# Row sums of a mixture of experts tied behind the last gate product, and three Hyena filters traced ahead of the projections

## The chip, the core and the metric

The kernel runs on one core of a Trainium2 chip. Its metric is the device time of one execution in microseconds (us): the median over several runs, beside one profiled execution whose trace is read below. Engines go by their short names: PE (TensorE, the matrix engine), DVE (VectorE), ACT (ScalarE), POOL (GpSimd), SP (SyncE, which issues most transfers).

## What is computed

Two layers of a trunk over 256 latent tokens (x) and 256 context tokens (xc), both 1024 wide. The layer's weights are shared by x and xc, and the modulation (six vectors from the conditioning c, through `ada_w`) differs between them. Cut to the parts that matter here:

```python
def _layer(x, xc, c, c_ctx, last, ...):
    sh1, sc1, g1, sh2, sc2, g2 = split(silu(c) @ ada_w + ada_b, 6)
    h = _rms(x, norm_mix) * (1.0 + sc1) + sh1
    q, k, v, hy, gates = _project(h, w_in, q_norm, k_norm)
    attn = _neighbourhood_attention(...)
    hyena = _hyena(hy, short_w, short_b, _hyena_filter_fft(L, flt_w1, ..., flt_w3), hy_skip)
    x = x + g1 * _merge(attn, hyena, gates, w_br_a, w_br_b, w_out)
    h2 = _rms(x, norm_ffn) * (1.0 + sc2) + sh2
    x = x + g2 * _hier_moe(h2, ...)          # 4 groups of 8 experts, top 1 group, top 2 experts
    if last: return x, xc                    # layer 1 needs of xc only keys and values
    ...                                      # the same for xc, with its own modulation

def _hier_moe(h, ...):                       # for each expert e and token t that it has
    y += (silu(h @ w1[e]) * (h @ w3[e]) * cw[t, e]) @ w2[e]
```

The Hyena filter does not depend on the tokens: a small sine network of the position, times a decay, normed over the positions, then a Fourier transform. There is one for each layer and order, (0,0), (0,1), (1,0) and (1,1).

## The kernel before, in words

All work is written by hand for the engines, in one program text that a tile library turns into one instruction stream for each engine. The order on an engine follows the place in the text, with a scheduler that moves an instruction past others when it is ready sooner; buffers come from numbered slots (`self.S(k, ...)`), and a transfer into a slot waits until the work on its last content is done.

**Start.** `build` loads constants and runs the filters' sine network (L1011), then loads eight 1 MB pieces of modulation weights (`ada_step`, L305): two at once, six inside `layer` through a ring of slots (L414). PE multiplies each piece with the conditioning as it lands (L316). `filter_load` (L1019) fetches the filters' weights, decay and Fourier table. `layer` then makes the rows of h: `head` (L441) squares x on ACT for its norm (L450), scales it (xn, L457), has PE transpose it (L461), ACT apply the modulation (hf) and DVE split it into a high and a low part (hT). `mm3` (L239 to L241) multiplies in three passes, high by high, low by high, high by low.

**A filter** (`filter`, L1035) has for each half of the positions two matmuls with decay (L1049, DVE hx), sums and differences (sf, half of them on POOL), splits (sd), absolute values (ACT) and their sum (ab, POOL), a norm matmul (L1063); then small matmuls for a reciprocal (L1069) and 24 three-pass matmuls of the Fourier transform, whose result H is stored to memory. Filter (0,0) stands behind `head`, the other three behind the projections of c = 0, 1, 2 (L550).

**The MoE** (`first_round`, L1373). Experts are worked on in 16 pairs. For a pair, `w13` (L1411) multiplies the pair's tokens with w1 and w3; `hidden` (L1359) makes the SiLU on ACT (sl), the gate product hd on DVE (L1365), a transpose on PE (L1368) and a copy on ACT (hdT); `w2` (L1426) follows. Weights stream in through rings of slots (`fetch`, L1390). The results of pairs 0 to 11 go out to rows of a buffer in memory (ybuf), the last four pairs' are put together by matmuls with a choice matrix (L1456). `collect(i)` (L1295) asks on POOL's queue for the two result rows of token tile i (yr or yt), and the function that it returns, `add`, sums them, multiplies by the modulation g2 and adds them to x, all three on DVE. Behind the first round stands a loop `overflow` for experts with more tokens than places; layer 1's head follows it.

The order around the change is set by the text, in `first_round`: half of the tiles is collected behind w2 of pair 12, their additions are written ahead of the second `hidden` from the end, and the other half is collected there and added at the end:

```python
            hdT = self.hidden(w13(2 * q, z["xT"], fill), z["cw"][:, 0:1])
            if q == 7:
                for u in adds:
                    u()
                adds = [collect(i) for i in range(nt // 2, nt)]
            ...
            if q == 6:
                adds = [collect(i) for i in range(nt // 2)]
```

## Time and profile before

| | us |
|---|---|
| median of 3 runs | 1447.03 (1446.01 to 1447.13) |
| the profiled execution | 1441.07 |
| its span in the trace | 1439.3 |
| busy: PE, DVE, ACT, POOL | 1281.0, 660.3, 455.8, 211.0 |
| first projection matmul starts | 59.39 |
| layer 0's MoE, last gate product | 867.42 |
| layer 1's first projection matmul | 893.28 |
| layer 1's MoE, last w2 starts | 1423.50 |

Times in a trace count from the span's start. The span is what the instructions of the core cover, the execution's own time lies 1.8 us over it. A row of a timeline has the start, the time, the engine (PEld is PE's weight load), the line, the operation, output and inputs; the brackets behind it tell how long the engine stood idle before it and what ended that. Matmuls are pipelined, so a row's time is longer than the distance to the next. A table by stretches gives busy time by engine, PE's granted clock as a share of 2.4 GHz, and the transfers' share of the 16 DMA engines.

### The profile page before, as it was taken

Reading aid. Unit: us, or ns where it says so; the run is one execution under the profiler, and the core shown is the slowest. Engines: PE = TensorE matmul, PEld = TensorE weight load, DVE = VectorE, ACT = ScalarE, POOL = GpSimd, SP = SyncE. Lnnn points to the kernel's source line nnn. Section 1 sums busy time; section 2 is a strip of 40 time slices with the busy share of each in tenths; the row PEclk is TensorE's granted clock in tenths of the full one; section 3 lists DMA queues with packets and bytes.
Section 4 is the critical chain, followed back from the end, with each engine's and each line's share of the span. In section 5 each row is a group of like instructions: output and inputs, shape, how many; then the busy total and the mean of one; then the engine's idle time right before and its main releaser. Section 6 shows DMA issues by size and latency. Waiting matters only on the chain. (4 is left out here: it accounts for less than half of the span.)

```text
span 1439.3 us, 18183 instructions
## 1 busy us (share of the span) xinstructions
PE 1281.0 (89%) x7071; PEld 831.1 (58%) x7071; DVE 660.3 (46%) x1361; ACT 455.8 (32%) x884; POOL 211.0 (15%) x175
## 2 busy tenths in 40 slices
PE   5999999999999999599888397999899969998776
PEld 2555777886578887344333134899779943443222
DVE  4654366676677666601000137865774760100014
ACT  3433223337632133222211014533574522221101
POOL 2021033361000000211110000032500021110000
PEclk9999999999999999699999699999999979999989
DMA  9744625455177762799999963325326749999991
GB/s 377 282 166 185 230 90 190 159 219 215 59 262 274 288 241 98 278 408 420 419 420 422 403 274 137 129 106 211 136 94 219 259 161 380 418 419 420 422 407 69
DMA packets 65691, 373.04 MB, mean 259 GB/s; under 512 B 11994, under 2 KB 13338, under 8 KB 26048
## 3 DMA queue, kind: packets, MB, share of 16 engines
q1 hardware_dynamic: 54368, 347.67, 61.9%
q0 software_dynamic: 10368, 21.02, 4.1%
q10 hardware_dynamic: 864, 3.15, 0.5%
q8 instruction: 57, 0.93, 0.3%
q14 instruction: 34, 0.28, 0.1%
HBM read 362.06 MB, written 27.53 MB: 271 GB/s over the span
## 5 line engine op out<-in xcount | busy, mean ns | idle before, releaser
L1411 PE MATMUL pW<-we,xT 128*64 128x512 f32 x1024 | 263.0, 605 | 8.5 <-DMA we<-in_wexp_dram 8.4
L1411 PEld LDWEIGHTS pW<-we,xT 128*64 128x64 f32 x1024 | 82.3, 138 | 149.8 <-issue 131.7
L239 PE MATMUL pA<-hT,wsp 128*128 128x512 f32 (+1 forms) x448 | 156.3, 349 | 4.0 <-ACT hf L223 4.0
L1365 DVE SCALAR_TENSOR_TENSOR hd<-sl,cws,pW 128x256 f32<-128x256 f32 x32 | 15.3, 480 | 305.9 <-ACT sl L223 305.9
L241 PE MATMUL pA<-hT,wsp 128*128 128x512 f32 (+1 forms) x448 | 154.4, 345 | 1.1 <-DVE wsp L220 1.1
L240 PE MATMUL pA<-hT,wsp 128*128 128x512 f32 (+1 forms) x448 | 154.0, 344 | 0.0
L220 DVE TENSOR_TENSOR wsp<-win,wsp 128x1024 fp32r<-128x1024 f32 x80 | 102.1, 1281 | 105.8 <-ACT wsp L223 105.6
L1426 PE MATMUL pW<-we,hdT 128*64 128x512 f32 x512 | 142.0, 621 | 4.9 <-ACT hdT L223 4.7
L223 ACT ACTIVATE wsp<-win 128x1024 fp32r<-128x1024 f32 x80 | 84.1, 1057 | 141.9 <-PE pA L241 137.2
L240 PE MATMUL pA<-wsp,hT 128*128 128x256 f32 x352 | 99.9, 284 | 2.6 <-DVE wsp L220 2.6
L239 PE MATMUL pA<-wsp,hT 128*128 128x256 f32 x352 | 100.2, 285 | 0.7 <-ACT vv L223 0.7
L241 PE MATMUL pA<-wsp,hT 128*128 128x256 f32 x352 | 99.7, 283 | 0.0
L239 PEld LDWEIGHTS pA<-hT,wsp 128*128 128x128 f32 x448 | 86.2, 192 | 21.6 <-issue 8.0
L240 PEld LDWEIGHTS pA<-hT,wsp 128*128 128x128 f32 x448 | 86.1, 192 | 13.7 <-issue 6.1
L241 PEld LDWEIGHTS pA<-hT,wsp 128*128 128x128 f32 x448 | 85.9, 192 | 11.1 <-issue 1.8
L1426 PEld LDWEIGHTS pW<-we,hdT 128*64 128x64 f32 x512 | 48.6, 141 | 73.3 <-issue 59.2
L223 ACT ACTIVATE Y<-pW 128x512 f32<-128x512 f32 (+1 forms) x64 | 38.2, 597 | 137.0 <-PE pW L1426 134.7
L223 ACT ACTIVATE sl<-pW 128x256 f32<-128x256 f32 x32 | 12.3, 383 | 218.7 <-PE pW L1411 218.7
L248 POOL TENSOR_TENSOR rs<-rsq,mh 128x1 f32<-128x1 f32 x14 | 8.4, 601 | 424.9 <-DVE rsq L247 414.0
L239 PEld LDWEIGHTS pA<-wsp,hT 128*128 128x128 f32 x352 | 67.3, 191 | 5.3 <-issue 2.5
L240 PEld LDWEIGHTS pA<-wsp,hT 128*128 128x128 f32 x352 | 67.4, 191 | 3.4 <-DVE wsp L220 3.2
L241 PEld LDWEIGHTS pA<-wsp,hT 128*128 128x128 f32 x352 | 67.4, 191 | 0.2
(301 smaller groups left out, 2324.4 us busy)
## 6 DMA issues: line engine op xcount, KB each, us to landing
we<-in_wexp_dram SPq DMA_DIRECT2D x190, 1024.0 KB
win<-in_win_dram SPq DMA_DIRECT2D x40, 1024.0 KB
ada<-in_ada_dram SPq DMA_DIRECT2D x32, 1024.0 KB
ada<-in_adaj_dram SPq DMA_DIRECT2D x16, 1024.0 KB
wbr<-in_wbr_dram SPq DMA_DIRECT2D x8, 1024.0 KB
wout<-in_wout_dram SPq DMA_DIRECT2D x8, 1024.0 KB
ybuf<-zero SPq DMA_DIRECT2D x12, 512.0 KB
bc<-modd SPq DMA_DIRECT2D x12, 512.0 KB
```

The costliest lines, as they stand in the source:

```text
L220: (eng or self.nc.vector).tensor_tensor(out=out, in0=a, in1=b, op=op)
L223: self.nc.scalar.activation(out, in_, func, **kw)
L239: self.nc.tensor.matmul(out, lh, rh, start=start, stop=False)
L240: self.nc.tensor.matmul(out, lh, rl, start=False, stop=False)
L241: self.nc.tensor.matmul(out, ll, rh, start=False, stop=stop)
L248: nc.gpsimd.tensor_tensor(out=out, in0=t, in1=self.mh[:, : shape[1]], op=ALU.pow)
L1365: nc.vector.scalar_tensor_tensor(out=hd, in0=sl, scalar=cws, in1=pa[:, 256:512], op0=ALU.mult, op1=ALU.mult)
L1411: nc.tensor.matmul(pa[64 * e : 64 * e + 64, :], xT[:, kc, cs], wt[(2 * p + e, kc // 4)][:, kc % 4, :], start=kc == 0, stop=kc == KC - 1)
L1426: nc.tensor.matmul(py[64 * e : 64 * e + 64, :], hdT[:, fc, 64 * e : 64 * e + 64], wt[(2 * p + e, 2)][:, fc, hs], start=fc == 0, stop=fc == 1)
```

## The change

Five edits. (1) In `build`, the filters' loads come first, the eight modulation pieces get slots of their own, and filters (0,0) and (0,1) are traced ahead of `layer`; (1,0) follows layer 0's `head`, (1,1) the projections of c = 0. (2) The output of the squares, which nobody reads, goes into xn in place of a buffer `sqj`. (3) H is stored through POOL's queue. (4) In the MoE only tiles 0 and 1 are collected, behind w2 of pair 12 and at once; POOL makes their sum and the product with g2, and the addition to x on DVE is tied behind the last gate product (`issue_after(self.last_hd)`). (5) In layer 0, the rows of tiles 2 and 3 (context) are asked for behind the first round, and POOL sums and multiplies them behind layer 1's `head([0, 1])`; DVE adds them in `head([2, 3])`. Layer 1's weight ring is one slot shorter in its last pass, since yr now has slot 15.

```diff
@@ build
-        for s in (4, 5):
+        self.filter_load(14, 16, 15)
+        for s in (4, 5, 6):
             self.ada_step(s)
-        self.filter_load(14, 16, 15)
         self.xres = self.load_x(20, 21)
+        for s in (7, 8, 9, 0, 1):
+            self.ada_step(s)
+        self.filter(0, 0, (17, 19), 2, "A", "B", "C")
+        self.filter(0, 1, (12, 13), 3, "A", "B", "C")
@@ layer
-        aring, ai = [6, 7, 8, 9, 12, 4, 5], [0]
+        aring, ai = [7, 8, 9, 4, 5, 6], [0]
...
                 if not full and i > 1:
+                    self.tt(xs[1][:, i % 2, :], xs[1][:, i % 2, :], self.crows[i - 2][0], ALU.add)
...
-                    j = self.T4([P, D], name="sqj")
-                    self.act(j, x_, AF.Square, accum_out=ss[:, 0:1])
+                    self.act(xn[i // 2][:, i % 2, :], x_, AF.Square, accum_out=ss[:, 0:1])
...
             head([0, 1])
+            y0, y1, gc = self.crows[0]
+            first = nc.gpsimd.tensor_tensor(out=y0, in0=y0, in1=y1, op=ALU.add).ins
+            with self.tc.issue_after(first):
+                self.tt(y0, y0, gc, ALU.mult, nc.gpsimd)
+                y0, y1, gc = self.crows[1]
+                self.tt(y0, y0, y1, ALU.add, nc.gpsimd)
+                self.tt(y0, y0, gc, ALU.mult, nc.gpsimd)
         if full:
-            self.filter(0, 0, (17, 19), 12, "B", "B", "C")
+            self.filter(1, 0, (17, 19), 20, "B", "B", "C")
...
-        for o in range(1 if full else 2):
+        for o in range(2):
...
             if c < 3 and full:
-                self.filter(*((0, 1), (1, 0), (1, 1))[c], (17, 19), 20, "B", "B", "C")
                 if c == 0:
-                    self.skip_load(1)
-                    self.tt(sw[:, 8:12, :], ...)
-                if c == 2:
+                    self.filter(1, 1, (17, 19), 20, "B", "B", "C")
+                if c == 0:
                     aring[:] = [14, 16, 18, 17, 19, 20, 21]
@@ filter_load
         self.skip_load(0)
+        self.skip_load(1)
@@ filter
-        nc.sync.dma_start(self.Hd[l, o], H.rearrange("p x j c -> p (x j c)"))
+        nc.gpsimd.dma_start(self.Hd[l, o], H.rearrange("p x j c -> p (x j c)"))
@@ moe, collect
-            if full and i % 2 == 0:
-                yr = self.S(21, [P, 2, D], name="yr")
+                yr = self.S(21 if full else 15, [P, 2, D], name="yr")
...
+            self.tt(yt[0], yt[0], yt[1], ALU.add, nc.gpsimd)
+            self.tt(yt[0], yt[0], g2[:, 0, :], ALU.mult, nc.gpsimd)
             def add():
-                x_ = xm[i // 2][:, i % 2, :]
-                self.tt(yt[0], yt[0], yt[1], ALU.add)
-                self.tt(yt[0], yt[0], g2[:, i // 2, :], ALU.mult)
-                self.tt(x_, x_, yt[0], ALU.add)
+                x_ = xm[0][:, i, :]
+                with self.tc.issue_after(self.last_hd):
+                    self.tt(x_, x_, yt[0], ALU.add)
@@ moe, behind the overflow loop
+        if full:
+            gc = self.T4([P, D], name="gc")
+            nc.sync.dma_start(gc, self.modd[l, 3, 1:2, :].partition_broadcast(P)[:, 0, :])
+            self.crows = []
+            for i in (2, 3):
+                yr = self.S((17, 19)[i - 2], [P, 2, D], name="yc")
+                for k in range(2):
+                    nc.gpsimd.dma_start(yr[:, k, :], ybuf[(k * nt + i) * P : (k * nt + i) * P + P, :])
+                self.crows.append((yr[:, 0, :], yr[:, 1, :], gc))
@@ first_round
-            seq = [15, 18, 11, 13, 16, 21, 2, 3, 17, 19, 4, 5, 6, 7, 8, 9] * 6
+            seq = [15, 18, 11, 13, 16, 21, 2, 3, 17, 19, 4, 5, 6, 7, 8, 9] * 5
+            seq += seq[1:16] + [18]
...
-            if q == 7:
-                for u in adds:
-                    u()
-                adds = [collect(i) for i in range(nt // 2, nt)]
...
             if q == 6:
-                adds = [collect(i) for i in range(nt // 2)]
+                adds = [collect(i) for i in range(2)]
```

Lines of the changed kernel lie a few below those of before: L1049 is L1058, L1063 is L1072, L1365 is L1384, L535 and L537 are L546 and L548, L316 and L354 are L320 and L358, L461 is L465.

**DVE, layer 0's MoE, the last pairs.** Before, hd of pairs 11, 12 and 13 (yr and yt are collected rows, the Y between are pair 12's results):

```order
L1365 SCALAR_TENSOR_TENSOR hd_6036<-sl_6034,cws_5463,pW_5990 128x256
L220 TENSOR_TENSOR yr_6133<-yr_6133 128x1024
L220 TENSOR_TENSOR yt_6136<-yt_6136,yt_6137 128x1024
L1365 SCALAR_TENSOR_TENSOR hd_6122<-sl_6120,cws_5630,pW_6076 128x256
L220 TENSOR_TENSOR Y_6129<-pW_6143,Y_6129 128x512
L220 TENSOR_TENSOR Y_6129<-pW_6152,Y_6129 128x512
L1365 SCALAR_TENSOR_TENSOR hd_6185<-sl_6183,cws_5630,pW_6140 128x256
L220 TENSOR_TENSOR Y_6192<-pW_6229,Y_6192 128x512
```

and, up to the hd of pair 15 (x is the residual stream, bc the modulation g2):

```order
L220 TENSOR_TENSOR yr_6272<-yr_6272 128x1024
L220 TENSOR_TENSOR yr_6272<-yr_6272,bc_6130 128x1024
L220 TENSOR_TENSOR yt_6275<-yt_6275,yt_6276 128x1024
L220 TENSOR_TENSOR x_4407<-x_4407,yr_6272 128x1024
L220 TENSOR_TENSOR yt_6275<-yt_6275,bc_6130 128x1024
L220 TENSOR_TENSOR x_4407<-x_4407,yt_6275 128x1024
L1365 SCALAR_TENSOR_TENSOR hd_6333<-sl_6331,cws_5797,pW_6280 128x256
```

Now, hd of pairs 14 and 15 and what follows:

```order
L1384 SCALAR_TENSOR_TENSOR hd_6259<-sl_6257,cws_5793,pW_6226 128x256
L220 TENSOR_TENSOR Y_6266<-pW_6270,Y_6266 128x512
L220 TENSOR_TENSOR Y_6266<-pW_6279,Y_6266 128x512
L1384 SCALAR_TENSOR_TENSOR hd_6320<-sl_6318,cws_5793,pW_6267 128x256
L220 TENSOR_TENSOR x_4400<-x_4400,yr_6129 128x1024
L220 TENSOR_TENSOR x_4400<-x_4400,yt_6134 128x1024
L220 TENSOR_TENSOR Y_6329<-pW_6340,Y_6329 128x512
L220 TENSOR_TENSOR Y_6329<-pW_6347,Y_6329 128x512
```

Two row sums stood ahead of the hd of pair 12 and six row operations of tiles 2 and 3 ahead of that of pair 15; now no row sum is on DVE, and the two additions to x stand directly behind the hd of pair 15.

**PE, ahead of layer 0's first projection.** Before, the last rows ahead of it and its own first (xn is transposed, hT and wsp are the projection's operands):

```order
L316 MATMUL pD_513<-ada_511,cc 32x512 x3
L1049 MATMUL pB_533<-w_19_163,fl_72 128x512
L461 MATMUL pA_320<-cst,xn_230 128x128 x2
L461 MATMUL pA_320<-cst,xn_231 128x128 x2
L461 MATMUL pA_329<-cst,xn_230 128x128 x2
L461 MATMUL pA_329<-cst,xn_231 128x128 x2
L1049 MATMUL pB_551<-w_19_163,fl_72 128x512
L1049 MATMUL pB_555<-w_19_163,fl_72 128x512
L239 MATMUL pA_441<-hT_226,wsp_438 128x512
```

Now, the end of the modulation (ada is a piece of its weights, L358 transposes its result) and what follows it; the first projection stands twelve rows behind the last one shown, transposes, a norm matmul and four of the next modulation between:

```order
L1058 MATMUL pB_525<-w_15_148,fl_72 128x512
L1058 MATMUL pB_529<-w_15_148,fl_72 128x512
L320 MATMUL pD_161<-ada_210,cc 32x512 x4
L1058 MATMUL pB_547<-w_15_148,fl_72 128x512
L1058 MATMUL pB_551<-w_15_148,fl_72 128x512
L358 MATMUL pD_217<-cst,md_162 128x128 x4
L1072 MATMUL pC_524<-ab_541,cst 128x512
L239 MATMUL pB_582<-sd_523,ft_152 128x512
L240 MATMUL pB_582<-sd_523,ft_152 128x512
L241 MATMUL pB_582<-sd_523,ft_152 128x512
L239 MATMUL pB_590<-sd_523,ft_152 128x512
L240 MATMUL pB_590<-sd_523,ft_152 128x512
```

Before, filter (0,0) and the four L1049 of (0,1) stood ahead of the first projection. Now all of (0,0) and (0,1) does, and of (1,0) the four L1058, both L1072 and six three-pass matmuls.

**DVE and POOL, layer 1's head.** DVE around the halves of the first u, before and now (yc are rows of tiles 2 and 3):

```order
L220 TENSOR_TENSOR qraw_7190<-cst,prm_6640 128x128
L535 SCALAR_TENSOR_TENSOR u_6729<-pA_6704,prm_6640,u_6729 128x255
L247 TENSOR_SCALAR rsq_6930<-ss_5013 128x1
L220 TENSOR_TENSOR qraw_7190<-cst,prm_6640 128x2x16
L537 SCALAR_TENSOR_TENSOR u_6729<-pA_6704,prm_6640,u_6729 128x255
L220 TENSOR_TENSOR wsp_6804<-win_6349,wsp_6804 128x1024
```

```order
L220 TENSOR_TENSOR hT_6634<-hf_6669,hT_6633 128x256
L546 SCALAR_TENSOR_TENSOR u_6724<-pA_6699,prm_6631,u_6724 128x255
L220 TENSOR_TENSOR x_4403<-x_4403,yc_6625 128x1024
L548 SCALAR_TENSOR_TENSOR u_6724<-pA_6699,prm_6631,u_6724 128x255
L220 TENSOR_TENSOR wsp_6799<-win_6332,wsp_6799 128x1024
L220 TENSOR_TENSOR vS_6695<-pA_6753,vS_6695 128x2x128
L546 SCALAR_TENSOR_TENSOR u_6758<-pA_6728,prm_6631,u_6758 128x255
L220 TENSOR_TENSOR x_4403<-x_4403,rest_6403 128x512
```

POOL behind the overflow loop, now:

```order
L1375 DMA yc_6625<-ybuf_124 128x1024 x2
L988 DMA ft_7190<-in_fmain_dram 128x2048
L481 TENSOR_TENSOR yc_6625<-yc_6625 128x1024
L220 TENSOR_TENSOR yc_6628<-yc_6628 128x1024
L220 TENSOR_TENSOR yc_6625<-yc_6625,gc_6623 128x1024
L220 TENSOR_TENSOR yc_6628<-yc_6628,gc_6623 128x1024
```

The addition of tile 2's rows stands between the two halves of the first u, and waits there for POOL's third row operation; before, POOL had only loads there and no 128x1024 operation.

## Rows read from the trace of the kernel before

**Rows 1.** Stretches: us, busy PE, PEld, DVE, ACT, POOL; PEclk, DMA share, GB/s.

```profile
160.00:580.00 420.00, 412.33 (x2372) 318.78 (x2370) 275.80 (x524) 151.52 (x304) 68.69 (x46) 1.00 0.52 191
780.00:800.00 20.00, 10.14 (x41) 3.42 (x37) 0.00 (x0) 2.07 (x4) 3.18 (x5) 0.86 1.02 420
800.00:820.00 20.00, 6.55 (x19) 2.21 (x19) 3.19 (x4) 1.07 (x3) 0.54 (x1) 0.54 0.98 405
1360.00:1380.00 20.00, 6.19 (x20) 2.33 (x17) 1.62 (x2) 0.77 (x2) 1.70 (x3) 0.61 1.02 422
```

**Rows 2.** Timeline of layer 0's MoE, 790 to 813 (start, us, engine, line; idle before).

```profile
790.17 0.38 ACT L223 ACTIVATE sl<-pW 128x256 f32<-128x256 f32 x1 [6.55 <-PE pW L1411]
...
803.78 1.23 DVE L220 TENSOR_TENSOR yr<-yr 128x1024 f32<-128x1024 f32 x1 [28.20 <-DMA yr<-ybuf]
...
812.44 0.48 DVE L1365 SCALAR_TENSOR_TENSOR hd<-sl,cws,pW 128x256 f32<-128x256 f32 x1
...
812.97 0.69 PE L1368 MATMUL pX<-cst,hd 128*128 128x128 f32 x2 [22.84 <-DVE hd L1365]
```

**Rows 3.** Layer 0, pairs 12, 14 and 15: timeline of PE, then one stretch.

```profile
814.14 5.72 PE L1426 MATMUL pW<-we,hdT 128*64 128x512 f32 x16 [0.47 <-ACT hdT L223]
...
849.37 0.44 PE L1368 MATMUL pX<-cst,hd 128*128 128x128 f32 x2 [0.99 <-DVE hd L1365]
...
850.28 3.71 PE L1426 MATMUL pW<-we,hdT 128*64 128x512 f32 x16 [0.47 <-ACT hdT L223]
...
867.95 0.44 PE L1368 MATMUL pX<-cst,hd 128*128 128x128 f32 x2 [3.39 <-DVE hd L1365]
...
844.00:846.00 2.00, 2.00 (x12) 0.64 (x10) 0.00 (x0) 0.00 (x0) 0.00 (x0) 1.00 0.04 16
```

**Rows 4.** Layer 1, pairs 12 to 15: timeline of PE and its weight loads, one stretch.

```profile
1376.11 0.69 PE L1368 MATMUL pX<-cst,hd 128*128 128x128 f32 x2 [13.81 <-DVE hd L1365]
...
1378.18 5.40 PE L1426 MATMUL pW<-we,hdT 128*64 128x512 f32 x15
...
1385.47 0.20 PEld L1411 LDWEIGHTS pW<-we,xT 128*64 128x64 f32 x4 [0.25 <-DMA we<-in_wexp_dram]
...
1423.50 3.65 PE L1426 MATMUL pW<-we,hdT 128*64 128x512 f32 x16
...
1408.00:1410.00 2.00, 1.01 (x6) 0.34 (x6) 1.05 (x2) 0.42 (x2) 0.00 (x0) 1.00 0.24 92
```

**Rows 5.** Start: timeline of PE and DVE, one stretch, groups of PE from 60 to 160.

```profile
20.01 2.08 PE L1049 MATMUL pB<-w,fl 64*128 64x512 f32 x4
...
49.97 0.68 DVE L220 TENSOR_TENSOR H<-pB,skb 128x512 f32<-128x512 f32 x1
...
59.39 0.50 PE L239 MATMUL pA<-hT,wsp 128*128 128x512 f32 x1
...
10.00:59.30 49.30, 40.82 (x174) 18.28 (x172) 28.75 (x66) 18.56 (x36) 9.39 (x9) 0.97 0.88 353
...
112.08 0.39 PE L239 MATMUL pB<-sd,ft 128*128 128x512 f32 x1
...
113.22 0.39 PE L241 MATMUL pB<-sd,ft 128*128 128x512 f32 x1
...
L1063 PE MATMUL pC<-ab,cst 128*128 128x512 f32 x12 | 6.8, 645 | 4.9 <-POOL ab L220 4.9
```

**Rows 6.** Layer 1's head: POOL group, row loads, DVE's splits (min/median/max), timeline.

```profile
L220 POOL TENSOR_TENSOR c<-qraw 128x512 f32<-128x512 f32 x2 | 4.0, 2000 | 0.0
...
yt<-ybuf POOLq DMA_DIRECT2D x8, 512.0 KB, 11.4
...
L220 DVE TENSOR_TENSOR wsp<-win,wsp x20: 1211/1225/2322, 887.8 to 998.4; 128x1024 fp32r<-128x1024 f32 x20
...
886.45 1.42 DVE L457 TENSOR_SCALAR xn<-x,rs 128x1024 f32<-128x1024 f32 x2 [0.58 <-DVEq L1350]
...
898.55 0.48 DVE L535 SCALAR_TENSOR_TENSOR u<-pA,prm,u 128x255 f32<-128x255 f32 x1 [0.94 <-ACT u L223]
```

More of the change, by code (lines that the diff above doesn't have):

```diff
@@ L543, in layer @@
             if c < 3 and full:
-                self.filter(*((0, 1), (1, 0), (1, 1))[c], (17, 19), 20, "B", "B", "C")
                 if c == 0:
-                    self.skip_load(1)
-                    self.tt(sw[:, 8:12, :], sw[:, 8:12, :], self.rn[0][:, 1, :].unsqueeze(2).to_broadcast([P, 4, 4]), ALU.mult)
-                if c == 2:
+                    self.filter(1, 1, (17, 19), 20, "B", "B", "C")
+                if c == 0:
                     aring[:] = [14, 16, 18, 17, 19, 20, 21]
@@ L1364, in hidden @@
         hd = self.TH([P, 256], name="hd")
-        nc.vector.scalar_tensor_tensor(out=hd, in0=sl, scalar=cws, in1=pa[:, 256:512], op0=ALU.mult, op1=ALU.mult)
+        self.last_hd = nc.vector.scalar_tensor_tensor(out=hd, in0=sl, scalar=cws, in1=pa[:, 256:512],
+                                                      op0=ALU.mult, op1=ALU.mult).ins
         ptt = self.ps("X", [P, 2, P])
```

## Prediction

> **What bounds the kernel now.** I read the page first: PE is by far the busiest engine, so time can come only from PE's gaps. The table by stretches shows where these are: PE is at 412.3 of 420 us from 160 to 580, but has 10.1 of 20 us from 780 to 800, 6.6 of 20 from 800 to 820 and 6.2 of 20 from 1360 to 1380, with its granted clock at 0.54 and 0.61 of 2.4 GHz there, close to the 1.2 GHz level [rows 1]. Then I read what ended each gap. In layer 0's MoE, ScalarE had the SiLU of pair 12 at 790.55, but DVE's gate product hd came only at 812.44: two 128x1024 sums stand ahead of it in DVE's order, and waited for rows that GpSimd had asked for (28.20 us for the first). PE stood 22.84 us for that hd [rows 2]. Layer 1 repeats it up to 1376.11, where PE stood 13.81 us [rows 4]. Last comes what the transfers allow: they run at 1.02 of their share through both gaps [rows 1], so weights keep arriving while PE stands, and that limits how far PE can move up.
>
> **B, the tail of layer 0's MoE.** The change takes every sum and product of MoE rows off DVE's order ahead of hd: at pair 12 nothing is left in front, and the last pair's six operations (two tiles, three each) are no longer there either. Three savings:
> - the wait itself, 22.8 us [rows 2];
> - half clock after it: w2 of pair 12 took 5.72 us, that of pair 14 3.71 [rows 3], so 2.0;
> - PE's wait for the last hd was 3.39 us against 0.99 at pair 14 [rows 3], so 2.4.
>
> Together 27.2. But the last hd cannot come before its weights. The transfer share is down to 0.04 in 844 to 846 [rows 3], so the last weights land near 845. The transfers were not standing in the gap, so I leave that time where it is. The transpose of the last hd then moves from 867.95 [rows 3] to about 846: **-22**. What PE could gain beyond, 5 us, becomes waits for weights.
>
> What it costs: the context rows (tiles 2, 3) are now asked for behind the routed part, two tiles summed and multiplied by GpSimd when layer 1 begins, and added to x by DVE between the two halves of layer 1's first u. That wait is new. Behind it on DVE are u's second half, a weight split and vS; PE waits for u with the transposes of projection 0, all its later projections standing behind them. The later pair of loads starts at about the loop's end, where the first xn stands (886.45 before), and lands 8 to 11 us later (11.4 is the median of yt) [rows 6], near 896. GpSimd has no 128x1024 sum in this trace; the longest of its 128x512 kinds takes 2.00 us [rows 6], so 2.0 to 4.0 at twice the columns; I take 3. The first needed product is the third in GpSimd's order: 896 + 3 x 3 = 905. Before, the u it splits stood at 898.55 [rows 6]. So DVE waits some 6 us there, of which PE can cover about a half with the next projection; DVE has 2.4 us fewer sums. I take **+3**, from -1 (the sums finish while xn and hT are made) to +8 (all of the wait reaches PE). Together **-19**, from -14 to -23.
>
> **C, the tail of layer 1's MoE.** The same sums leave DVE ahead of hd of pair 12: 13.8 us of wait, and 15 of the w2 matmuls behind it took 5.40 at half clock against 3.65 us for 16 of the last pair [rows 4]: 1.8. Sum 15.6. Against it stand the weights: at 1385.47 PE's load for pair 13 waited for a weight even in the delayed order [rows 4], and the share reaches 0.24 only in 1408 to 1410 [rows 4]. The last w2 ran from 1423.50; with weights in at about 1411 it can move by 12.5 at most. One row transfer more is put ahead of them (four row loads now go out together, against two at pair 12 and one at pair 13): 0.5 MB, 1.25 us at the 420 GB/s of those rows [rows 1]. **-11**, from -5 (a pair held twice by weights) to -12.5.
>
> **A, the start.** Three filters of Hyena are put ahead of the projections in the trace. By the order, filter (0,1) stands wholly ahead of the first projection matmul, of (1,0) its four decay matmuls, two norms and six three-pass matmuls; before, (0,0) stood there and four matmuls of (0,1). PE's price for one filter: four of L1049 at 1.04 (two, in four records, took 2.08), 4.2; two of L1063 at 1.13 (6.8 us for six), 2.3; 24 three-pass ones 0.23 apart (six starts from 112.08 to 113.22), 5.5; eight small ones of L1069 at the same spacing, 1.8 [rows 5]. That is 13.8. So 9.6 of (0,1) and 4.2 + 2.3 + 1.4 of (1,0), 17.5 us, pass from behind the first projection to ahead of it. They cost nothing where they fill PE's idle time there: 49.3 - 40.8 = 8.5 us between 10 and 59.3 [rows 5]. So the first projection moves from 59.39 by at least 9.0 us. At most it moves by 17.5 and the waits of filters with little beside them, which I bound by 5: three times a filter's share of PE's waits for the norm's input in 60 to 160, 4.9 / 3 [rows 5]. Of those 4.9 us, six norms of three filters, four norms leave: 3.3. So the sum is 9.0 - 20.8 = -11.8 at best and 22.5 - 20.8 = +1.7 at worst. I take a shift of 14.8, a little under the middle because matmuls of the modulation stand between the filters': **-6**.
>
> **Priced at nothing.** The square's output that goes into xn: ScalarE, same size. H's stores on GpSimd's queue in place of SP's: four issues of 1 MB, SP freed for weights. Loads of the modulation weights into slots of their own: the transfers before the first projection are the same bytes but for 0.5 MB of skip weights.
>
> **Sum.** -6 - 19 - 11 = -36. The profiled execution took 1441.07, so 1405. That execution lies 6.0 under the median of the runs, 1447.03; on that scale the time is **1411**.
>
> **A rule weighed.** What the row shows: the weight splits on DVE in layer 1's head take 1.225 us, and the longest of 20 took 2.322 [rows 6]. The Trainium skill's "SBUF — State Buffer", section "SBUF: two separate sides", says that a DVE operation with two SBUF inputs and a GpSimd operation that reads SBUF share one port pair, as a lock held for the whole instruction. The single long row agrees with such a lock, though it does not prove it. The time by such blocking is rival 3.
>
> **Rivals.**
> 1. *Weights bind both tails.* For: the wait of pair 13's load on a weight, and transfers at their full share. Every pair would stand a little for its weights, at the lower clock. Then B gives -12 and C -6: 1447 - 6 - 12 - 6 = 1423. Against: in layer 0 the last weights are in some 20 us before the last hd [rows 3]. Chance 0.14.
> 2. *The start gives nothing.* A filter is a chain PE, DVE, GpSimd and ScalarE, PE, and two more of them have only modulation matmuls to hide behind. A at +2: 1447 + 2 - 30 = 1419. Chance 0.13.
> 3. *GpSimd's sums block DVE in layer 1's head.* Four of 3 us make 12 us in which DVE's own sums and splits would stand still; with the 3 already counted, 8 to 9 more: 1419. For: the 2.322 us row. Against: the median split is 1.225, though GpSimd worked less there. Chance 0.12.
> 4. *Slower.* At the start the filters run as serial chains, each as long as (0,0) did: from 20.01 to its last H at 49.97, 30 us [rows 5]. Two more in a row move the first projection by 60, less the 20.8 that leave later stages: +39, against -30 of the tails: 1456. It decides from a first projection later than 110 us. Against: PE was at work 40.8 of 49.3 us there, on the modulation too. Chance 0.03.
> 5. *The sums still stand in front,* because the tie holds only what it names. Then only A stays, 1441, or nothing if A gives nothing. Against: the order has both x additions right behind hd of pair 15 and no row sum on DVE ahead of it. Chance 0.02.
>
> **How the numbers follow.** My forecast has 0.56. The low end takes all three parts at their best, -11.8 - 23 - 12.5 = -47, so 1400, and 3 for the measurement: 1397. The high end takes rival 1's 1423 and 3 more for it with a poor start: 1426. What a measurement can tell from no change is about 0.2%, 2.9 us. Slower is rival 4, 0.03; for no change I put rival 5's 0.02, though A alone would be a little faster; the rest, 0.95, is faster.
>
> **What would show it.** Right: hd of pair 12 half a microsecond behind its SiLU in both layers; PE's longest wait for hd under 3 us; no stretch from 780 to 820 under 15 us of PE; the last hd of layer 0 some 28 us earlier with the start's part, and end-of-weights waits of PE in place of the wait for hd; DVE standing about 6 us for a GpSimd product in layer 1's head; the first projection near 74. Wrong: PE waiting over 10 us for weights in either tail, a first projection past 82, splits on DVE over 2 us beside GpSimd's sums, or layer 1's first transposes of u more than 10 us behind the first projection.

## The result and the profile after

The changed kernel took 1423.62 us (median of 4 runs, 1421.39 to 1430.05), the kernel before 1446.52 beside it: ratio 0.9853, 95% interval 0.9817 to 0.9889. So it is faster by 1.5%, within the range forecast, but 12.6 us above the 1411 forecast. The profiled execution took 1422.41 us, 18.7 under the profiled one of before; the forecast sum was 36.

The page of the changed kernel, busy time by engine (us, share of the span, instructions):

```profile
PE 1278.2 (90%) x7071; PEld 832.5 (59%) x7071; DVE 652.4 (46%) x1349; ACT 457.3 (32%) x884; POOL 245.0 (17%) x191
```

PE has as much to do as before (1281.0), so the whole gain is idle time that went. Where it went is read by comparing starts of the same instruction in the two traces, the **lead**. First the stretches of the changed kernel (columns as in [rows 1]); the first and last belong to the start and layer 1's head:

```profile
10.00:79.40 69.40, 56.76 (x234) 27.14 (x235) 45.47 (x85) 30.54 (x56) 23.51 (x18) 0.98 0.74 292
...
780.00:800.00 20.00, 18.46 (x73) 6.74 (x71) 1.86 (x3) 3.65 (x7) 3.17 (x5) 1.00 1.01 419
800.00:820.00 20.00, 15.94 (x58) 5.39 (x55) 1.87 (x3) 1.96 (x4) 4.68 (x2) 1.00 1.01 411
...
860.00:880.00 20.00, 9.98 (x65) 8.46 (x64) 9.27 (x27) 5.95 (x11) 9.58 (x8) 0.82 0.54 193
...
1360.00:1380.00 20.00, 15.10 (x55) 5.06 (x55) 1.41 (x3) 1.97 (x4) 4.67 (x2) 0.91 1.02 418
```

The two holes of before are closed: PE has 18.5 and 15.9 us in 780 to 820 (10.1 and 6.6 [rows 1]) at full clock. A new hole stands in 860 to 880.

Timeline, the start, layer 0's tail and layer 1's tail of the changed kernel:

```profile
16.01 2.07 PE L1058 MATMUL pB<-w,fl 64*128 64x512 f32 x2 [3.77 <-ACT fl L223]
...
79.40 0.80 PE L239 MATMUL pA<-hT,wsp 128*128 128x512 f32 x1
...
790.91 0.38 ACT L223 ACTIVATE sl<-pW 128x256 f32<-128x256 f32 x1 [6.54 <-PE pW L1432]
...
791.33 0.48 DVE L1384 SCALAR_TENSOR_TENSOR hd<-sl,cws,pW 128x256 f32<-128x256 f32 x1 [15.01 <-ACT sl L223]
...
805.79 3.65 PE L1432 MATMUL pW<-we,xT 128*64 128x512 f32 x14 [2.59 <-DMA we<-in_wexp_dram]
...
844.85 0.44 PE L1388 MATMUL pX<-cst,hd 128*128 128x128 f32 x2 [0.99 <-DVE hd L1384]
...
1001.31 0.38 PE L240 MATMUL pA<-wsp,hT 128*128 128x256 f32 x1 [1.19 <-DVE wsp L220]
...
1352.91 0.38 ACT L223 ACTIVATE sl<-pW 128x256 f32<-128x256 f32 x1 [8.14 <-PE pW L1432]
...
1353.33 0.48 DVE L1384 SCALAR_TENSOR_TENSOR hd<-sl,cws,pW 128x256 f32<-128x256 f32 x1 [15.22 <-ACT sl L223]
...
1364.13 8.77 PE L1432 MATMUL pW<-we,xT 128*64 128x512 f32 x30 [3.33 <-DMA we<-in_wexp_dram]
...
1404.59 3.65 PE L1447 MATMUL pW<-we,hdT 128*64 128x512 f32 x16
```

Seven starts give the ledger (a positive lead is time by which the changed kernel is ahead):

| place (before, after) | lead | step |
|---|---|---|
| first projection (59.39, 79.40) | -20.0 | |
| SiLU of pair 12, layer 0 (790.17, 790.91) | -0.7 | start: 0.7 lost |
| last hd transposed, layer 0 (867.95, 844.85) | 23.1 | layer 0's tail: 23.8 gained |
| layer 1's first projection (893.28, 867.65) | 25.6 | 2.5 gained |
| an L240 matmul of wsp by hT (1013.50, 1001.31) | 12.2 | layer 1's head: 13.4 lost |
| SiLU of pair 12, layer 1 (1362.33, 1352.91) | 9.4 | 2.8 lost |
| last w2 (1423.50, 1404.59) | 18.9 | layer 1's tail: 9.5 gained |

The tails did what was forecast, and the start gave nothing. The loss is in layer 1's head. Its timeline in the changed kernel:

```profile
867.65 0.39 PE L239 MATMUL pA<-hT,wsp 128*128 128x256 f32 x1 [1.40 <-ACT hf L223]
871.43 0.48 DVE L546 SCALAR_TENSOR_TENSOR u<-pA,prm,u 128x255 f32<-128x255 f32 x1 [1.26 <-ACT u L223]
872.61 2.36 POOL L481 TENSOR_TENSOR yc<-yc 128x1024 f32<-128x1024 f32 x1 [8.31 <-DMA yc<-ybuf]
874.94 2.33 POOL L220 TENSOR_TENSOR yc<-yc 128x1024 f32<-128x1024 f32 x1
877.24 4.63 POOL L220 TENSOR_TENSOR yc<-yc,gc 128x1024 f32<-128x1024 f32 x2
879.60 3.35 DVE L220 TENSOR_TENSOR x<-x,yc 128x1024 f32<-128x1024 f32 x1 [7.68 <-POOL yc L220]
883.49 0.68 PE L524 MATMUL pA<-cst,u 128*128 128x128 f32 x2 [9.82 <-DVE u L548]
...
892.94 1.22 DVE L220 TENSOR_TENSOR x<-x,yc 128x1024 f32<-128x1024 f32 x1
```

Read it downwards. GpSimd's three operations in front of DVE's addition (two sums and the first of the two products in the row at 877.24) end at about 879.6; DVE has stood 7.68 us for them between the halves of u. The addition then takes 3.35 us beside GpSimd's second product, while the second addition (892.94), with no GpSimd work beside it, takes 1.22. Only then comes u's second half, and PE stands 9.82 us for it.

### The profile page after: what moved, and what is told of

It reads as the page before. It is cut to its first block, busy times and chain, and to the rows that moved or that the text cites. A ratio compares the mean times of both kernels' runs of the same rounds, so it can differ in the third digit from the quotient of the medians.

```text
span 1420.6 us, 18183 instructions
## 1 busy us (share of the span) xinstructions
PE 1278.2 (90%) x7071; PEld 832.5 (59%) x7071; DVE 652.4 (46%) x1349; ACT 457.3 (32%) x884; POOL 245.0 (17%) x191
## 5 line engine op out<-in xcount | busy, mean ns | idle before, releaser
L1432 PE MATMUL pW<-we,xT 128*64 128x512 f32 x1024 | 263.1, 605 | 16.3 <-DMA we<-in_wexp_dram 15.6
L1384 DVE SCALAR_TENSOR_TENSOR hd<-sl,cws,pW 128x256 f32<-128x256 f32 x32 | 15.4, 481 | 354.1 <-ACT sl L223 354.1
L240 PE MATMUL pA<-hT,wsp 128*128 128x512 f32 (+1 forms) x448 | 154.2, 344 | 0.0
L1447 PE MATMUL pW<-we,hdT 128*64 128x512 f32 x512 | 137.2, 598 | 4.9 <-ACT hdT L223 4.7
L240 PE MATMUL pA<-wsp,hT 128*128 128x256 f32 x352 | 100.5, 286 | 2.5 <-DVE wsp L220 2.5
L240 PEld LDWEIGHTS pA<-hT,wsp 128*128 128x128 f32 x448 | 86.2, 192 | 13.2 <-issue 5.5
L241 PEld LDWEIGHTS pA<-hT,wsp 128*128 128x128 f32 x448 | 86.1, 192 | 10.7 <-issue 1.3
L240 PEld LDWEIGHTS pA<-wsp,hT 128*128 128x128 f32 x352 | 68.2, 194 | 3.3 <-DVE wsp L220 3.1
```

The source lines that it names most:

```text
L240: self.nc.tensor.matmul(out, lh, rl, start=False, stop=False)
L241: self.nc.tensor.matmul(out, ll, rh, start=False, stop=stop)
L1384: self.last_hd = nc.vector.scalar_tensor_tensor(out=hd, in0=sl, scalar=cws, in1=pa[:, 256:512], op0=ALU.mult, op1=ALU.mult).ins
L1432: nc.tensor.matmul(pa[64 * e : 64 * e + 64, :], xT[:, kc, cs], wt[(2 * p + e, kc // 4)][:, kc % 4, :], start=kc == 0, stop=kc == KC - 1)
L1447: nc.tensor.matmul(py[64 * e : 64 * e + 64, :], hdT[:, fc, 64 * e : 64 * e + 64], wt[(2 * p + e, 2)][:, fc, hs], start=fc == 0, stop=fc == 1)
```

## Experiments

All are edits of the changed kernel ("after" below, 1423.62). Three groups ran beside the kernel before, at 1444.27, 1444.55 and 1446.40 us; ratios are against it, so they compare across groups. Differences in us below are of medians. Taken from the ratios, experiment 4 lies 6.7 us under after (7.6 by the medians), and experiments 7 and 9 lie 4.0 and 4.5 over 4 (4.8 and 5.1). First each part alone.

**1. The start undone:** filters, modulation slots, the squares' output and H's stores as before; tails and layer 1's head as changed.

```diff
@@ build
-        self.filter_load(14, 16, 15)
-        for s in (4, 5, 6):
+        for s in (4, 5):
             self.ada_step(s)
+        self.filter_load(14, 16, 15)
         self.xres = self.load_x(20, 21)
-        for s in (7, 8, 9, 0, 1):
-            self.ada_step(s)
-        self.filter(0, 0, (17, 19), 2, "A", "B", "C")
-        self.filter(0, 1, (12, 13), 3, "A", "B", "C")
...
```

> The change without its start: filters, modulation slots, the squares' output and H's stores as before; the MoE parts stay. Theory (the 17.5 us of filter work came to stand ahead of the first projection, but filled none of PE's idle time there, so the start is worth 0 to 2 us): first projection near 59.4 in place of 79.4, the tails and layer 1's head as in the changed kernel, time 1421 to 1427, within 3 us of the changed kernel's 1423.6. Rival (the start is worth the 6 us of the prediction and something else in layer 0 took them back): 1429 to 1431.

Measured: 1423.69 us, ratio 0.9857 (0.9841 to 0.9874), as the whole change. The start is worth nothing; the 20 us by which the first projection is later come back behind it, and no more.

**2. Layer 1's tail undone:** sums, products and additions on DVE again, called ahead of the second-last hidden.

```diff
@@ moe, collect
-            self.tt(yt[0], yt[0], yt[1], ALU.add, nc.gpsimd)
-            self.tt(yt[0], yt[0], g2[:, 0, :], ALU.mult, nc.gpsimd)
+            if full:
+                self.tt(yt[0], yt[0], yt[1], ALU.add, nc.gpsimd)
+                self.tt(yt[0], yt[0], g2[:, 0, :], ALU.mult, nc.gpsimd)
             def add():
                 x_ = xm[0][:, i, :]
+                if not full:
+                    self.tt(yt[0], yt[0], yt[1], ALU.add)
+                    self.tt(yt[0], yt[0], g2[:, 0, :], ALU.mult)
+                    self.tt(x_, x_, yt[0], ALU.add)
+                    return
@@ first_round
             if q == 7:
+                if not full:
+                    for u in adds:
+                        u()
...
```

> The changed kernel with layer 1's row sums, products and additions on DVE again, ahead of the second last gate product in the text, so that both sums stand ahead of hd of pair 12; layer 0 stays as changed. Theory (layer 1's tail is worth 9 to 10 us, and comes from this order alone): DVE waits for the rows ahead of hd of pair 12, PE stands 12 to 18 us there, time 9 to 13 us over the changed kernel, 1432 to 1437. Rival (weights bound that tail, the lead of 19 us at its end was the lead at its start): under 3 us, 1421 to 1427.

Measured: 1441.54 us (8 runs), ratio 0.998 (0.9969 to 0.9991), 18 over after. Timeline of this kernel, DVE and PE:

```profile
1370.87 1.23 DVE L220 TENSOR_TENSOR yr<-yr 128x1024 f32<-128x1024 f32 x1 [27.51 <-DMA yr<-ybuf]
1378.52 1.23 DVE L220 TENSOR_TENSOR yt<-yt,yt 128x1024 f32<-128x1024 f32 x1 [6.42 <-DMA yt<-ybuf]
1379.66 0.48 DVE L1390 SCALAR_TENSOR_TENSOR hd<-sl,cws,pW 128x256 f32<-128x256 f32 x1
...
1380.19 0.69 PE L1394 MATMUL pX<-cst,hd 128*128 128x128 f32 x2 [22.12 <-DVE hd L1390]
```

The row sums ahead of hd cost what PE waits for them. It is more than expected because two tiles are now asked for at once, so two sums stand there: the second waits another 6.42 us for its rows. In the kernel before it was one:

```profile
1374.43 1.23 DVE L220 TENSOR_TENSOR yt<-yt,yt 128x1024 f32<-128x1024 f32 x1 [26.72 <-DMA yt<-ybuf]
```

The rival, that weights hold this tail anyway, falls.

**3. Rows asked for later:** the four row loads go out from ScalarE's queue behind the SiLU of pair 13; the load of g2 stays where it was.

```diff
@@ moe, collect
             for k in range(2):
-                nc.gpsimd.dma_start(yt[k], ybuf[(k * nt + i) * P : (k * nt + i) * P + P, :])
+                with self.tc.issue_after(self.sls[-2]):
+                    nc.scalar.dma_start(yt[k], ybuf[(k * nt + i) * P : (k * nt + i) * P + P, :])
...
```

> The changed kernel with the row loads of the two tiles issued from ScalarE's queue behind the SiLU of pair 13 in place of behind w2 of pair 12, in both layers. Theory (2 MB of rows go ahead of the weights of pair 13, 5 us at 420 GB/s, and make PE's 3.3 us wait for weights and its lower clock in layer 1, 2.6 us in layer 0): both waits go under 1 us, time 3 to 6 us lower, 1418 to 1421. Rival (the end of all weights bounds the tails, rows and weights together take the same time in either order): within 2 us, 1421 to 1426.

Measured: 1423.39 us, ratio 0.9847 (0.9827 to 0.9867), no change. Timeline of PE in this kernel, layer 1, pairs 13 and 15:

```profile
1365.46 7.08 PE L1436 MATMUL pW<-we,xT 128*64 128x512 f32 x30 [0.88 <-DMA we<-in_wexp_dram]
...
1395.17 5.40 PE L1436 MATMUL pW<-we,xT 128*64 128x512 f32 x16 [4.24 <-DMA we<-in_wexp_dram]
```

The wait for weights at pair 13 went from 3.33 to 0.88 us and came back as 4.24 at pair 15. With the sums out of the way, the tail ends with the last transfer, whichever goes first: the rival held.

Now layer 1's head.

**4. The additions later:** both context additions are tied behind the last half of u of projection 3.

```diff
@@ layer, head
-                    self.tt(xs[1][:, i % 2, :], xs[1][:, i % 2, :], self.crows[i - 2][0], ALU.add)
+                    with self.tc.issue_after(self.last_u):
+                        self.tt(xs[1][:, i % 2, :], xs[1][:, i % 2, :], self.crows[i - 2][0], ALU.add)
@@ layer, behind the second half of u
...
+                if m < 4:
+                    self.last_u = last
```

> The changed kernel with the two additions of the context rows in layer 1's head tied behind the last half of u of projection 3, nothing else moved by hand. Theory (DVE's wait of 7.7 us for GpSimd's products, the 3.35 us addition beside a GpSimd product, and PE's 9.8 us and lower clock behind them are the 15 us that layer 1's head lost): PE's wait ahead of the first transposes of u goes from 9.8 to under 1.5, 8 to 12 us come back, time 1411 to 1416. Rival (the head's time comes back as a wait for weights in layer 1's MoE, or DVE's later work only moves behind the projections): at most 3 us, 1420 to 1424.

Measured: 1416.01 us (1414.3 to 1416.69), ratio 0.9807 (0.979 to 0.9823): 7.6 under after, and 7.7 under experiment 1, which ran in the same group. That is a little under the theory's 8 to 12 us, and far from the rival's 3. Timeline of PE, DVE and POOL in this kernel:

```profile
866.09 0.58 PE L239 MATMUL pA<-hT,wsp 128*128 128x256 f32 x1 [1.15 <-ACT hf L223]
...
872.06 2.52 DVE L220 TENSOR_TENSOR wsp<-win,wsp 128x1024 fp32r<-128x1024 f32 x1
...
873.47 3.38 POOL L220 TENSOR_TENSOR yc<-yc 128x1024 f32<-128x1024 f32 x1
...
875.62 2.31 DVE L220 TENSOR_TENSOR wsp<-win,wsp 128x1024 fp32r<-128x1024 f32 x1
...
878.97 2.31 DVE L220 TENSOR_TENSOR wsp<-win,wsp 128x1024 fp32r<-128x1024 f32 x1
...
887.62 0.48 PE L525 MATMUL pA<-cst,u 128*128 128x128 f32 x2 [1.74 <-DVE u L549]
894.93 1.12 PE L466 MATMUL pA<-cst,xn 128*128 128x128 f32 x4 [4.07 <-DVE rsq L247]
...
993.49 0.39 PE L240 MATMUL pA<-wsp,hT 128*128 128x256 f32 x1 [1.20 <-DVE wsp L220]
```

PE's wait for u fell from 9.82 to 1.74 us, so the place of the additions was the largest part of the head's loss. But from the first projection to the row at 993.49 the lead still falls from 27.2 to 20.0, and the weight splits on DVE now take 2.3 to 2.5 us beside GpSimd's work. Two suspects are left: that blocking, and DVE's load.

**5. All context row work on DVE:** as 4, but sums and products are on DVE too, tied at the same place.

```diff
@@ layer, head
...
+                    y0, y1, gc = self.crows[i - 2]
                     with self.tc.issue_after(self.last_u):
+                        self.tt(y0, y0, y1, ALU.add)
+                        self.tt(y0, y0, gc, ALU.mult)
                         self.tt(xs[1][:, i % 2, :], xs[1][:, i % 2, :], y0, ALU.add)
@@ layer, behind head([0, 1])
-            first = nc.gpsimd.tensor_tensor(out=y0, in0=y0, in1=y1, op=ALU.add).ins
...
```

> As the experiment with the additions tied behind the projections' u (1416.0), but sums and products of the context rows on DVE too, all tied there; GpSimd does no row work in layer 1's head. DVE has 4 x 1.22 = 4.9 us more to do in front of the context's xn. Theory (what that version still loses in layer 1's head, about 8 us of lead against the ends of the two tails, is DVE's chain in front of the context's xn): PE's wait for that xn grows from 4.1 by 2 to 5 us, time 1418 to 1421. Rival (the loss there is GpSimd's blocking of DVE's splits): no weight split in the head over 1.5 us, the wait does not grow, time 1413 to 1416.

Measured: 1417.16 us (1415.8 to 1421.4), ratio 0.9811 (0.9795 to 0.9827), the same as 4. Timeline of DVE and PE in this kernel:

```profile
871.80 1.23 DVE L220 TENSOR_TENSOR wsp<-win,wsp 128x1024 fp32r<-128x1024 f32 x1
...
874.95 1.23 DVE L220 TENSOR_TENSOR wsp<-win,wsp 128x1024 fp32r<-128x1024 f32 x1
...
878.12 1.23 DVE L220 TENSOR_TENSOR wsp<-win,wsp 128x1024 fp32r<-128x1024 f32 x1
...
894.80 1.11 PE L469 MATMUL pA<-cst,xn 128*128 128x128 f32 x4 [6.25 <-DVE xn L465]
...
899.28 1.12 PE L469 MATMUL pA<-cst,xn 128*128 128x128 f32 x4 [3.37 <-DVE xn L465]
```

The same three splits take 1.23 us each: the blocking is gone, as the rival said, and with it PE's 1.74 us for u. But PE's wait for the context's xn grew from 4.07 to 9.62 us (two waits), as the theory said. The time lies between the two forecasts, at neither. Stretch 880 to 900 in experiment 4 (columns as in [rows 1]):

```profile
880.00:900.00 20.00, 13.81 (x82) 11.43 (x81) 19.48 (x34) 9.42 (x21) 7.43 (x6) 0.83 0.49 174
```

and in experiment 5:

```profile
880.00:900.00 20.00, 10.38 (x69) 9.15 (x68) 19.46 (x31) 7.77 (x17) 3.47 (x3) 0.82 0.24 79
```

DVE is at work 19.5 of 20 us in both. In the kernel before, without the context's row work, a stretch 7 to 27 us behind the first projection (here it is 14 to 34) had DVE at 17.3 and PE at 18.5:

```profile
900.00:920.00 20.00, 18.52 (x142) 16.85 (x140) 17.30 (x39) 11.49 (x21) 0.00 (x0) 1.00 0.45 159
```

So DVE was nearly full here already, and work that is moved here costs, on DVE directly or on GpSimd through DVE's longer operations. No run takes the row work out of this head again, so that DVE's load makes the rest of the loss is inferred, not shown.

**6. Products on DVE:** as after, with the addition where the change has it, but the product with g2 on DVE ahead of it.

```diff
@@ layer, head
+                    y0, y1, gc = self.crows[i - 2]
+                    self.tt(y0, y0, gc, ALU.mult)
                     self.tt(xs[1][:, i % 2, :], xs[1][:, i % 2, :], self.crows[i - 2][0], ALU.add)
@@ layer, behind head([0, 1])
-                self.tt(y0, y0, gc, ALU.mult, nc.gpsimd)
                 y0, y1, gc = self.crows[1]
                 self.tt(y0, y0, y1, ALU.add, nc.gpsimd)
-                self.tt(y0, y0, gc, ALU.mult, nc.gpsimd)
```

> The changed kernel, but the products of the context rows with g2 are made on DVE, directly ahead of their additions; GpSimd only sums. In the changed kernel the two sums ended at 877.24 (layer 1's head), two GpSimd products of 2.3 us followed (both in a row of 4.63), and DVE's first addition stood from 879.60 for 3.35 us, against 1.22 for the second, which had no GpSimd work beside it. Theory 1 (DVE stands still while GpSimd works on two operands in SBUF): DVE's product starts when the first sum is there but is not done before the second sum ends, about 877.3 + 1.2; the addition then takes 1.22 and ends near 879.7 instead of 882.95, so PE's wait for u falls from 9.8 to about 6.6 us and the time by 3: about 1420.5. Theory 2 (no blocking, the addition was long for another reason): product from 875.0 at 1.2 us, addition done at 877.4, PE's wait about 4.3, time about 1418. Rival (what PE gains there it loses again waiting for the xn of the context tiles): time 1422 to 1424 with the shorter wait.

Measured: 1419.88 us (1417.36 to 1422.68), ratio 0.9824 (0.9808 to 0.984), as theory 1 forecast. Timeline of this kernel:

```profile
877.65 2.33 POOL L220 TENSOR_TENSOR yc<-yc 128x1024 f32<-128x1024 f32 x1
...
877.72 3.35 DVE L220 TENSOR_TENSOR yc<-yc,gc 128x1024 f32<-128x1024 f32 x1 [5.47 <-POOL yc L483]
...
881.33 1.21 DVE L220 TENSOR_TENSOR x<-x,yc 128x1024 f32<-128x1024 f32 x1
881.46 0.58 PE L240 MATMUL pA<-hT,wsp 128*128 128x256 f32 x1 [5.63 <-DVE hT L220]
```

The blocking moves with GpSimd: DVE's product, started 0.07 us behind GpSimd's second sum, takes 3.35 us, and the addition, now without GpSimd beside it, 1.21. Against the forecast, PE now stands for hT (5.63 us), which is queued behind the product, and not for u.

**7. Rows in another slot:** as 4, but tile 2's rows go into slot 12, so that they are loaded and summed ahead of the overflow loop, and the tie is one projection earlier.

```diff
-            first = nc.gpsimd.tensor_tensor(out=y0, in0=y0, in1=y1, op=ALU.add).ins
...
+            with self.tc.issue_after(self.last_row):
+                first = nc.gpsimd.tensor_tensor(out=y0, in0=y0, in1=y1, op=ALU.add).ins
...
-                if m < 4:
+                if m < 3:
...
-                yr = self.S((17, 19)[i - 2], [P, 2, D], name="yc")
+                yr = self.S((12, 19)[i - 2], [P, 2, D], name="yc")
...
```

> The kernel e3 with tile 2's rows in slot 12 in place of 17, which the overflow loop uses, so that they are asked for before the loop; both row sums on GpSimd are queued behind the row loads, ahead of the loop; the additions are tied behind u of projection 2. Theory (what is left of the head's loss is the chain from the context rows over the additions, the norm and xn to PE, where PE stood 4.1 us in e3): that wait falls under 1.5 us, time 1411 to 1414. Rival (the additions beside GpSimd's products take 2 to 3 us each by the lock, and give it back): within 1.5 us of e3, 1414.5 to 1417.5.

Measured: 1420.84 us, ratio 0.9835 (0.9815 to 0.9855), 4.8 slower than 4; both expectations fail. Timeline of this kernel:

```profile
852.81 2.40 POOL L483 TENSOR_TENSOR yc<-yc 128x1024 f32<-128x1024 f32 x1 [7.19 <-DMA yc<-ybuf]
853.05 4.38 DVE L220 TENSOR_TENSOR wsp<-win,wsp 128x1024 fp32r<-128x1024 f32 x2
...
865.10 1.42 DVE L462 TENSOR_SCALAR xn<-x,rs 128x1024 f32<-128x1024 f32 x2 [0.25 <-DVEq L1363]
...
870.97 4.86 POOL L220 TENSOR_TENSOR yc<-yc,gc 128x1024 f32<-128x1024 f32 x2 [3.15 <-DMA gc<-modd]
871.07 2.55 DVE L220 TENSOR_TENSOR hT<-hf,hT 128x256 fp32r<-128x256 f32 x1
873.54 2.64 DVE L230 CAST hT<-hf 128x256 fp32r<-128x256 f32 x2
```

The early sum sits beside two splits (4.38 us for both), and xn starts at 865.10 against 860.43 in 4. Of that, 2.3 us stood already at the SiLU of pair 12 in layer 0 (791.92 against 789.62), ahead of all that this edit moves, so some 2.4 us belong to it. The products sit beside the hT that PE needs at once, where the last addition of hT takes 2.55 us (0.42 elsewhere). Earlier rows gain nothing when GpSimd's work then lies beside DVE's critical one.

Last, three versions of the start, all with the additions later as in 4.

**8. The start undone** (edits of 1 and 4 together).

> The kernel e3 (additions of the context rows tied behind u of projection 3) with the start as before, too. Theory (the start is worth nothing by itself, also where layer 1's head no longer stands): within 3 us of e3's 1416.0, 1413 to 1419. Rival (the start is worth 6 us that layer 1's head had taken back): 1421 to 1423.

Measured: 1416.91 us, ratio 0.9807 (0.9782 to 0.9832), equal to 4. Again the start is worth nothing.

**9. Two modulation pieces ahead of the filters' loads.**

```diff
-        self.filter_load(14, 16, 15)
-        for s in (4, 5, 6):
+        for s in (4, 5):
             self.ada_step(s)
+        self.filter_load(14, 16, 15)
         self.xres = self.load_x(20, 21)
-        for s in (7, 8, 9, 0, 1):
+        for s in (6, 7, 8, 9, 0, 1):
```

> The kernel e3 with the first two modulation pieces loaded ahead of the filters' loads, as before the change; the filters stay ahead of the projections. Theory (in the changed kernel PE stood 3.8 us for ScalarE's part of the sine network between 10 and 20, where before two pieces of the modulation filled that wait; this is a large part of the 4 us by which PE's idle time ahead of the first projection grew): the wait falls under 1.5 us, the first projection comes 2 to 4 us earlier than 79.4, time 1412 to 1415. Rival (the filters' loads then land later and PE stands for the decay matmuls instead): within 1.5 us of e3, 1414.5 to 1417.5.

Measured: 1421.11 us, ratio 0.9838 (0.9818 to 0.9857), 5.1 slower than 4; both expectations fail. Timeline of PE in this kernel:

```profile
80.42 2.08 PE L1075 MATMUL pC<-ab,cst 128*128 128x512 f32 x2 [4.96 <-POOL ab L220]
...
87.41 0.63 PE L239 MATMUL pA<-hT,wsp 128*128 128x512 f32 x1
```

PE has more work during the filters' sine network (its longest wait there is 2.21 us in place of 3.77), but it stands 4.96 us for a filter's absolute sums later, and the first projection moves from 79.71 to 87.41. Only in part is that a loss: 21 more matmul records stand ahead of it (256 against 235 from 10 on). Also, this profiled execution is the fastest of its four (1417.12, 2.8 over that of 4), so the rows need not hold the whole 5.1 us; its cause is not settled.

**10. One filter ahead:** as 9, with only (0,0) ahead; (0,1) follows layer 0's head, (1,0) and (1,1) the projections of c = 0 and 1.

```diff
-        self.filter(0, 1, (12, 13), 3, "A", "B", "C")
...
-            self.filter(1, 0, (17, 19), 20, "B", "B", "C")
+            self.filter(0, 1, (17, 19), 20, "B", "B", "C")
...
-                if c == 0:
-                    self.filter(1, 1, (17, 19), 20, "B", "B", "C")
+                if c < 2:
+                    self.filter(1, c, (17, 19), 20, "B", "B", "C")
...
```

> The kernel e8 with only filter (0,0) ahead of layer 0's head; (0,1) behind the head, (1,0) and (1,1) behind the projections of c = 0 and 1. Theory (a filter with few matmuls beside it costs PE as much waiting as one between projections saves, so how many stand ahead makes no difference): first projection 8 to 12 us earlier than in e8, time within 2 us of e8. Rival (each filter ahead costs PE some 2 us of waits): 2 to 4 us under e8.

Measured: 1415.5 us (1413.4 to 1416.57), ratio 0.9796 (0.9774 to 0.9818), 5.6 under 9, more than the rival's 2 to 4, and no different from 4 and 8. The first projection starts at 75.56. With that order of loads the second filter ahead costs 5.6 us; with the change's own order two filters ahead cost nothing (4 against 8). Experiments 4, 5, 8 and 10 are the fastest versions measured, 6 to 8 us under the change, and their intervals do not tell them apart.

## Why the prediction was right or wrong

**Which waits would go** was right, and by its own signs: hd of pair 12 starts 0.04 us behind the end of its SiLU in both layers, no wait of PE for hd in the tails is over 0.99 us, and 780 to 820 has 18.5 and 15.9 us of PE, both over 15. Two of its signs of being right did not come, a first projection near 74 (79.40) and layer 0's last hd some 28 us earlier (23.1), and one of its signs of being wrong did: layer 1's first transposes of u stand 883.49 - 867.65 = 15.8 us behind the first projection, and 10 was the limit.

**B, layer 0's tail: right.** -22 was forecast, 23.8 was gained. The bound by the weights was real, but a little smaller than put: of the 27.2 us, 2.59 and 0.22 came back as waits for weights (the last of them ends at 840.21), not 5. That the last hd is transposed at 844.85, close to "about 846", does not confirm that its weights land near 845. Rival 1 would have given 12.

**C, layer 1's tail: right.** -11 forecast, 9.5 measured. Of the 15.6 us, 3.33 came back as PE's wait for weights at pair 13, and 1.7 as that pair's matmuls in 8.77 instead of 7.08 us (the granted clock is 0.91 in 1360 to 1380). Experiment 2 shows that the sums were the cause, experiment 3 that the transfers are what is left.

**B's other half, layer 1's head: the step that failed.** +3 was put, with a bound of +8; the ledger gives -2.5 + 13.4 + 2.8 = +13.7. DVE's wait itself was nearly right (6 us forecast, 7.68 measured, although GpSimd's operation takes 2.33 us and not 3). Wrong was "of which PE can cover about a half with the next projection": PE covered 1.8 us, for DVE stands from 871.9 and PE runs out of work at 873.7. Next in PE's order come projection 0's transposes of u, whose second half stands behind the addition on DVE; PE stood 9.82 us for them, and the projection behind them follows at once. Left out of the sum was that the addition would be blocked: 3.35 us against 1.22, 2.1 more. That is rival 3's mechanism, which the prediction had set beside the single long split of [rows 6] and priced, but kept out of its forecast and its +8. Experiment 4 gives back 7.6 us by the place of the additions alone. It leaves a loss of 7.2 us up to the row at 993.49; on the way, in 880 to 900, DVE is busy 19.5 of 20 us. The context's row work came from a tail in which DVE was mostly idle (1.86 of 20 us at work in 780 to 800) into a head in which it was nearly full (17.3 of 20 before). The prediction looked for what would wait there, not for how full DVE was. Of the 2.8 us that the changed kernel lost behind 1001.31 only a place is known: where q and k are prepared, up to the row at 1020.11, PE's waits for DVE and ScalarE come to 5.2 us (the longest 3.12), against 3.1 before. No run isolates it, so its cause stays open.

**A, the start: wrong by its size.** -6 was forecast, 0.7 was lost in the trace, and experiments 1 and 8 give nothing at all: rival 2. The runs carry this, not the 0.7: the changed kernel and experiments 4 and 7 have the same work up to pair 12 of layer 0, and its SiLU starts at 790.91, 789.62 and 791.92. The step is "I take a shift of 14.8". It was 20.0, near the bad end of the range given (22.5): PE's idle time ahead of the first projection was not filled but grew, from 49.3 - 40.8 = 8.5 to 69.4 - 56.8 = 12.6 us. PE stands 3.77 us for the sine network at 16.01, where two pieces of modulation stood before, and a little at each norm. The 20.8 us that were to come back behind were nearly all there: 20.0 - 0.7 = 19.3.

So on the scale of the profiled executions the error of 17.3 us is the head's 10.7, the start's 6.7, C's 1.5, and 1.8 the other way in B. On the medians 12.6 is left, because before's profiled execution lay 6.0 under its median and that of the changed kernel 1.2. That the time is inside the forecast's range is in part luck: its high end was rival 1's 1423 and 3 more, and rival 1 did not come. What came was rival 2, and a head 10.7 us worse than put.

## What to carry to other kernels

A sum that waits for late rows must not stand ahead of a gate product in an engine's order; taking it out gave 23.8 of 27.2 and 9.5 of 15.6 us, and part of the rest became waits for weights. Where it is moved to, first read how busy its engine is there and what is queued behind it: the same rows cost 14 us in a head whose DVE was nearly full, and half of that was the place of the additions. Tracing independent work early pays only if other work covers its chains; here PE's idle time ahead of the projections grew with it.

## What the runs showed of the hardware

DVE operations of two SBUF operands are held up by GpSimd operations on SBUF, until the GpSimd operation that runs beside them ends. One 128x1024 operation on DVE: 1.22 us alone, 3.35 where it met one GpSimd operation of 2.33 (after and experiment 6), and three splits of 2.52, 2.31 and 2.31 with GpSimd at work against 1.23 each without (experiments 4 and 5). GpSimd is held up too: its sum between two of these splits took 3.38 us (experiment 4), against 2.33 in the changed kernel. The Trainium skill's "SBUF — State Buffer", section "SBUF: two separate sides", says that the two share one port pair as an exclusive lock for a whole instruction. Experiment 6 agrees: GpSimd's sum ends at 877.65 + 2.33 = 879.98, and 1.22 later would be 881.20; DVE's product ended at 881.07. Experiment 7 adds small ones: an hT addition of 2.55 instead of 0.42 us, and two casts, with one operand, in 2.64 instead of 0.49.
